# Layer A of a hybrid decoder step written out in TensorE's order

## The chip, the cores and the metric

The kernel runs as one program on one core of a Trainium2 chip. Its engines are TensorE (PE, with weight loads shown as PEld), VectorE (DVE), ScalarE (ACT), GpSimd (POOL) and SyncE (SP), which issues nearly all transfers between memory and the chip. The metric is the time of one execution on the device in microseconds (us), the median of the runs.

## The reference

One step of a two-layer decoder for a prompt of 272 positions (16 learned ones and 256 given) and 8 samples of one position. Layer A is RWKV-7 time mixing, layer B is sliding-window attention with a K/V shared from the stream after layer A. All is float32.

```python
prev = concat([shift_prev, xn[:, :-1]]); xx = prev - xn
xm = xn[:, :, None] + xx[:, :, None] * mu                       # six mixes of width 2048
r, k, v, z = einsum('btpd,pde->btpe', xm[:, :, :4], w_rkvz)      # 2048 x 4096 each
decay = exp(-exp(-softplus(-(w0 + tanh(xw @ w1) @ w2)) - 0.5)); a = sigmoid(a0 + (xa @ a1) @ a2)
kk = normalised(k * k_k); k = k * (1 + (a - 1) * k_a); b = kk * a
S = S * d - (S @ kk) b + v k; y = S @ r                          # scan over positions, 64 heads of 64
y = groupnorm(y) * gn_g + gn_b + sum(r * k * r_k) * v
h = x + (y * silu(z)) @ w_out                                    # 4096 x 2048
# layer B: shared K/V = rmsnorm(h) @ w_kv; q, z = rmsnorm(h) @ w_qz; attention with sinks;
# h = h + (att * silu(z)) @ w_o; out = rmsnorm(h)
```

## The kernel before, in words

A large product is computed as three products of rounded halves: weights and activations are split into a high part in TensorE's faster float32 form (fp32r) and the rest (`split`, L165: ACT makes the high part, DVE the rest), and `mm3` (L187) multiplies high by high, high by low and low by high. Weights come in pieces of 256 KB (`wunits`, L170: four raw buffers, five of each half); a piece serves 12 matmuls of 128 x 128 by 280 columns (272 prompt positions and 8 samples). A product here means one such sum for 256 output columns (`gemm`, L193): 8 pieces for 2048 inputs. Products go to one of three PSUM banks (`pm`).

The mixes for r, k, v and z are kept in memory (`md`), 8 tiles of 560 KB each, and loaded into a pool of 8 tiles (`load_mix`, L454). `proj` (L462) makes the products of one of r, k, v, z for some pairs of heads' blocks, evacuates them, and stores them to memory. k also gets the norms of its keys (`key_norms`), v is transposed.

Layer A has 64 heads, worked on in 16 units of four heads (u) and 8 double units (o). `prep` (L597) loads a unit's r, k, v, makes the decays and a (a small lora product each), and sends the samples' vectors to memory by a transpose (`ps_sm`, L664). `scores` (L707) makes the triangular products within chunks of 64 positions, `solve` (L769) inverts them in blocks (`ps_so`), `chain` (L838) passes the state through 5 chunks, each in three steps (ps_wu and ps_sy; the inverse, L888; the new state, L891 and L893), `group_norm` (L917) finishes y and stores it in `yd`. `decode` (L948) does the samples.

`phase_a` (L535) writes these in a loop over double units and puts the recurrence under `high_priority`; the products of the next group of heads (k, v and r, with three mix loads: nine in all, and one for z) stand between. Which instruction goes where on an engine is planned at build time by a scheduler that goes by simulated times and priorities, on TensorE too, so products and recurrence are interleaved by its plan. After the loop come the z products. For blocks below `GZ` = 14 pairs the z product is multiplied by y at once (L491 to L496); the last block is gated later (`gate_a`). `out_a1` (L1084) adds the first half of the output product (16 of 32 input tiles, blocks 0 to 3), with its gated y in mix tiles; `out_a` (L1107) loads and splits the late gates (`load_gated`, blocks 4 to 7) and does the second half. The scratch pool of the recurrence closes before `out_a` opens its own.

Of the kernel before, what the change touches and what calls it, by code (L numbers as in the profile page):

```python
# [8 lines left out]
F32 = mybir.dt.float32  # L9
# [20 lines left out]
LR = 96  # L30
HD = 64
NU = NP // 2
GZ = 14
# [65 lines left out]

class Kernel:  # L100
    def __init__(self, nc, tc, I, O):
        self.nc, self.tc, self.I, self.O = nc, tc, I, O

        self.raws, self.los = [], []

        self.wx = None
        self.plan = []

    def run(self):
        nc, tc = self.nc, self.tc  # L110
        import contextlib
        with contextlib.ExitStack() as st:
# [10 lines left out]
            with tc.tile_pool(name="stage", bufs=2) as self.sp:  # L123
                self.right = tc.tile_pool(name="mix", bufs=8, side="right")
                self.mp = self.right.__enter__()
                with tc.tile_pool(name="ph0", bufs=1) as self.ph:
                    self.phase0()
                with tc.tile_pool(name="rec", bufs=1, reuse_waits="tile") as self.rp:
                    self.phase_a()
            with tc.tile_pool(name="res", bufs=1, reuse_waits="tile") as self.op:  # L130
                self.right.__exit__(None, None, None)
                self.right = tc.tile_pool(name="kv", bufs=1, reuse_waits="tile", side="right")
                self.kvp = self.right.__enter__()
                self.right2 = tc.tile_pool(name="st0", bufs=1, reuse_waits="tile", side="right")
                self.st0 = self.right2.__enter__()
                self.right3 = self.tc.tile_pool(name="wx0", bufs=1, reuse_waits="tile", side="right")
                self.wx0 = self.right3.__enter__()
                with tc.tile_pool(name="gA", bufs=1, reuse_waits="tile") as self.gp:
                    self.out_a()
                with tc.tile_pool(name="B", bufs=1, reuse_waits="tile") as self.bp:  # L140
                    self.phase_b()
                with tc.tile_pool(name="gB", bufs=1, reuse_waits="tile") as self.gp:
                    self.out_b()
                self.wx = None
                self.right2.__exit__(None, None, None)
                self.right3.__exit__(None, None, None)
                self.g0.__exit__(None, None, None)
# [39 lines left out]
    def mm3(self, ps, wh, wl, xh, xl, start, stop):  # L187
# [3 lines left out]
        mm(ps, wl, xh, start=False, stop=stop)  # L191
# [95 lines left out]
    def phase0(self):  # L287
# [144 lines left out]
        self.xr0 = x(xr)  # L432
# [21 lines left out]
    def load_mix(self, m, nm):  # L454

        out = [self.mix_tile(f"{nm}_{g}") for g in range(8)]
        for t, d in zip(out, (self.md[m][g] for g in range(8))):
            self.nc.sync.dma_start(t.bitcast(F32), d)
        return lambda k: self.parts(out, k)


    def proj(self, m, x, pairs, dst, gemm=None):  # L462

        nc = self.nc
        for p0 in pairs:
# [5 lines left out]
            for j, ps in enumerate(pss):  # L471
                if m == 3:
                    th = self.sp.tile([128, N], F32, tag="sqp", bufs=1, name=f"th{p0}_{j}")
                    nc.scalar.activation(th, ps, AF.Tanh, scale=0.5)
                    nc.vector.scalar_tensor_tensor(t[:, j], th, 1.0, ps, op0=ALU.add, op1=ALU.mult)
                else:
                    nc.scalar.copy(t[:, j], ps)
                if m == 1:
                    sq = self.sp.tile([128, N], F32, tag="sqp", bufs=1, name=f"sqp{p0}_{j}")
                    nc.scalar.activation(sq, ps, AF.Square, scale=self.pcol(P_KK, p0 + j))  # L480
                    if j == 0:
                        pk = self.bank(self.py if p0 < 8 else self.pm, f"ps_kk{p0}")
                    nc.tensor.matmul(pk[:4, :N], self.sel[:, 4 * j:4 * j + 4], sq, start=j == 0, stop=j == 1)
                if m == 2:
                    pt = self.bank(self.pe if p0 < 8 else self.pm, name=f"ps_vt{p0}_{j}")
# [5 lines left out]
            if m == 3 and p0 < 2 * GZ:  # L491

# [345 lines left out]
    def chain(self, o):  # L838
# [17 lines left out]
        for q in range(2):  # L856
            G.memset(X[0][H(q), q], 0.0)
# [650 lines left out]
```

## Time and profile before

| | |
|---|---|
| median of 3 runs | 2351.3 us (2350.19 to 2351.96) |
| the profiled execution | 2355.23 us, of which the span from first to last instruction is 2352.6 us |
| busy share of the span | PE 96%, PEld 88%, DVE 73%, ACT 55%, POOL 3% |
| mean granted clock of TensorE | 0.981 |
| DMA | 464.71 MB, mean 198 GB/s |

Busy shares are means over stages. Layer A's products and recurrence lie between about 165 and 1410 us, the second output part and the shared K/V up to 1600, attention with the products of layer B from 1600 to 2100, the last product after that. Matmuls are pipelined: one of 280 columns is shown as about 0.29 us, and the next starts after less than half of that.

### The profile page before, as it was taken

How to read it: one execution, taken by the hardware profiler on the slowest of the kernel's cores; microseconds unless marked ns; L12 is line 12 of the kernel's file. 1: busy time of each engine (PE TensorE's matmuls, PEld its weight loads, DVE VectorE, ACT ScalarE, POOL GpSimd, SP SyncE). 2: the span in 40 equal slices, each digit the busy share in tenths (PEclk: the TensorE clock that was granted, in tenths of full speed). 3: DMA queues.
4: the chain of work that ended last, by engine and by line, in shares of the span. 5: the costliest groups of instructions: out<-in, count | busy, mean ns of one | idle time of the engine just before them, and what ended most of it. 6: DMA issues, size and time to landing. Idle time of an engine off the chain costs nothing.

```text
span 2352.6 us, 57011 instructions
## 1 busy us (share of the span) xinstructions
PE 2264.2 (96%) x21840; PEld 2069.3 (88%) x21840; DVE 1727.6 (73%) x4134; ACT 1299.4 (55%) x3042; POOL 63.5 (3%) x82
## 2 busy tenths in 40 slices
PE   7999999999999999999998999999999999999997
PEld 4898889888888888999898899999888899899997
DVE  5866768757785687876788567896777777688886
ACT  3556656665655766576554544564545445555443
POOL 0010000001000000000000000100000000000000
PEclk9999999999999999999999999999999999999999
DMA  7987667657586577855655568757343444356774
GB/s 251 327 262 255 208 211 250 214 184 248 150 244 213 167 230 226 258 172 155 196 168 163 168 193 263 242 185 224 108 129 117 144 131 137 110 170 219 233 226 148
DMA packets 425984, 464.71 MB, mean 198 GB/s; under 512 B 64472, under 2 KB 381336, under 8 KB 425320
## 3 DMA queue, kind: packets, MB, share of 16 engines
q1 hardware_dynamic: 424896, 458.79, 61.5%
q8 instruction: 171, 2.80, 0.5%
q10 hardware_dynamic: 816, 2.29, 0.3%
q14 instruction: 101, 0.83, 0.1%
HBM read 396.66 MB, written 68.44 MB: 198 GB/s over the span
## 4 chain that ended last, share of the span: by engine, by line
PE 83%; DMA 7%; DVE 5%; ACT 3%; issue 2%; SPq 0%; DVEq 0%; ACTq 0%
PE ps_z L189 6%; PE ps_z L190 6%; PE ps_z L191 6%; PE ps_q L191 3%; PE ps_q L189 3%; PE ps_q L190 3%; PE ps_ob L191 3%; PE ps_ob L190 3%; PE ps_ob L189 3%; PE ps_v L189 3%; PE ps_v L190 2%; PE ps_v L191 2%; PE ps_r L191 2%; PE ps_r L189 2%; PE ps_r L190 2%; PE ps_oa L191 2%
## 5 line engine op out<-in xcount | busy, mean ns | idle before, releaser
L167 ACT CAST whi_z<-raw_z 128x512 fp32r<-128x512 f32 x256 | 157.6, 619 | 151.0 <-PE ps_z L190 93.1
L168 DVE TENSOR_TENSOR wlo_z<-raw_z,whi_z 128x512 fp32r<-128x512 f32 x256 | 174.9, 691 | 72.3 <-ACT whi_z L167 64.0
L189 PE MATMUL ps_z<-mhlz,whi_z 128*128 128x280 f32 x512 | 153.5, 300 | 0.0
L190 PE MATMUL ps_z<-mhlz,whi_z 128*128 128x280 f32 x512 | 152.1, 298 | 0.0
L191 PE MATMUL ps_z<-mhlz,wlo_z 128*128 128x280 f32 x512 | 150.3, 297 | 0.0
L189 PE MATMUL ps_z<-bmh,whi_z 128*128 128x264 f32 x512 | 148.2, 291 | 0.0
L190 PE MATMUL ps_z<-bml,whi_z 128*128 128x264 f32 x512 | 148.0, 290 | 0.0
L191 PE MATMUL ps_z<-bmh,wlo_z 128*128 128x264 f32 x512 | 147.6, 292 | 0.0
L190 PE MATMUL ps_q<-bml,whi_q 128*128 128x264 f32 x512 | 147.4, 289 | 0.0
L189 PE MATMUL ps_q<-bmh,whi_q 128*128 128x264 f32 x512 | 147.3, 289 | 0.0
L191 PE MATMUL ps_q<-bmh,wlo_q 128*128 128x264 f32 x512 | 146.6, 289 | 0.0
L189 PE MATMUL ps_ob<-ghi,whi_ob 128*128 128x264 f32 x512 | 145.8, 286 | 0.3 <-ACT whi_ob L167 0.3
L191 PE MATMUL ps_ob<-ghi,wlo_ob 128*128 128x264 f32 x512 | 144.2, 285 | 1.7 <-DVE wlo_ob L168 1.7
L190 PE MATMUL ps_ob<-glo,whi_ob 128*128 128x264 f32 x512 | 145.6, 285 | 0.0
L167 ACT CAST whi_oa<-raw_oa 128x512 fp32r<-128x512 f32 x128 | 78.9, 621 | 91.1 <-PE ps_oa L190 57.0
L167 ACT CAST whi_q<-raw_q 128x512 fp32r<-128x512 f32 x128 | 78.6, 620 | 84.0 <-PE ps_q L190 57.2
L167 ACT CAST whi_ob<-raw_ob 128x512 fp32r<-128x512 f32 x128 | 79.0, 620 | 80.4 <-PE ps_ob L190 71.7
L168 DVE TENSOR_TENSOR wlo_oa<-raw_oa,whi_oa 128x512 fp32r<-128x512 f32 x128 | 86.6, 689 | 49.5 <-ACT whi_oa L167 46.9
L168 DVE TENSOR_TENSOR wlo_r<-raw_r,whi_r 128x512 fp32r<-128x512 f32 x128 | 87.2, 689 | 47.8 <-ACT whi_r L167 46.6
L189 PE MATMUL ps_k<-mhlk,whi_k 128*128 128x280 f32 x384 | 117.9, 308 | 3.1 <-issue 3.1
L167 ACT CAST whi_v<-raw_v 128x512 fp32r<-128x512 f32 x128 | 78.4, 619 | 71.8 <-PE ps_v L190 32.0
L189 PE MATMUL ps_r<-mhlr,whi_r 128*128 128x280 f32 x384 | 115.8, 303 | 1.9 <-ACT whi_r L167 1.7
(476 smaller groups left out, 7773.6 us busy)
## 6 DMA issues: line engine op xcount, KB each, us to landing
raw_k<-a_w_rkvz SPq DMA_DIRECT2D x128, 256.0 KB
raw_v<-a_w_rkvz SPq DMA_DIRECT2D x128, 256.0 KB
raw_r<-a_w_rkvz SPq DMA_DIRECT2D x128, 256.0 KB
raw_z<-a_w_rkvz SPq DMA_DIRECT2D x128, 256.0 KB
raw_oa<-a_w_out SPq DMA_DIRECT2D x128, 256.0 KB
raw_q<-b_w_qz SPq DMA_DIRECT2D x128, 256.0 KB
raw_z<-b_w_qz SPq DMA_DIRECT2D x128, 256.0 KB
raw_ob<-b_w_o SPq DMA_DIRECT2D x128, 256.0 KB
```

The costliest lines, as they stand in the source:

```text
L167: self.nc.scalar.copy(hi, src)
L168: return self.nc.vector.tensor_tensor(lo, src, hi.bitcast(F32), op=ALU.subtract)
L189: mm(ps, wh, xh, start=start, stop=False)
L190: mm(ps, wh, xl, start=False, stop=False)
L191: mm(ps, wl, xh, start=False, stop=stop)
```

## The change

The changed kernel writes layer A in the order that TensorE is to follow. `drive` holds TensorE's order by hand (`pe_order`) and counts half pieces: after each six product matmuls it looks at the streams `epilogues`, `main` (scores, solve and chain), `preps`, `decodes` and `late_gates`, plus group norms and even scores put aside. Each stream is a generator that gives the number of half pieces until its next visit, and a condition, and stands until both hold. The other engines are still planned by the scheduler; instructions of the side streams are queued on DVE behind the split of a recent weight piece.

- The products are a single stream: r for group 0, then r, k, v, then v, k, r, then r, k, v, then z, then the first output part. Neighbours with the same mix share it, so that mixes are loaded 7 times, not 10; tile h of the next mix is loaded after piece h of the last product that uses the old one.
- Weights are split three pieces ahead (`W`).
- In `prep` the lora products come ahead of the loads of r and k; v is loaded later; lora halves have two buffers.
- The mean and variance of the group norm are made in three parts within the chain (`variance`).
- `GZ` is 12, not 14: blocks 6 and 7 are gated late. The late gates are made in the stream `late_gates`, beside the first output part, in a pool that takes the place of the recurrence's early scratch.
- Pools are opened and closed by name; `res` lies on the right side, and `at` is made later.

```diff
-GZ = 14
+GZ = 12
-        for o in range(-1, NU // 2):
-            n = 2 * o + 2
-            if n < NU:
-                if n % 4 == 0 and n:
-                    self.proj_group(n // 4)
-                    self.decode(n // 4 - 1)
...
+        self.drive(self.products(), [self.epilogues(), self.main(), self.preps(), self.decodes(), self.late_gates()])
+    def drive(self, products, streams):
...
+        with self.pe_order():
+            while more or self.later or len(live) > 1:
+                for s in list(live):
+                    if s[1] <= self.pos and (s[2] is None or s[2]()):
+                        turn = self.tc.issue_after(self.los[-2].ins) if self.pos and s[0] not in now else \
+                            contextlib.nullcontext()
...
+                            with self.tc.high_priority(offset=2000 if s[0] is now[1] else 0), turn:
+                                w = next(s[0])
...
+                        s[1:] = [self.pos + w, need]
+                more = more and next(products, None) is not None
+                self.pos += 1
+    def main(self):
+        for o in range(-1, NU // 2):
+            n = 2 * o + 2
+            if o >= 0:
+                yield from self.chain(o)
+                self.mark('u', o)
+                self.side.append(self.group_norm(o))
+            if n < NU:
+                yield 0, self.after(0, ('p', n + 1), ('c', n))
+                self.load_x(o + 1)
+                self.prep_e(n + 1)
+                self.mark('e', n + 1)
+                yield from self.scores(n + 1)
+                yield from self.solve(o + 1)
+                self.mark('s', o + 1)
+    def products(self):
+        order = [(1, (0, 1, 2)), (2, (2, 1, 0)), (3, (0, 1, 2))]
...
+                while len(W) < 3:
+                    u = next(units, None)
...
+                for c in (0, 1):
+                    for k in (0, 1):
...
+                        self.last = self.mm3(ps[c][:, :N], wh[:, k, cs], wl[:, k, cs], xh, xl, k0 + k == 0,
+                                             k0 + k == KT - 1)
...
+                        if m < 4:
+                            mix[h] = self.mix_part(m, h, i)
+                        else:
+                            mix[h] = self.gated1(h, ys.pop(0))
...
+                    yield True
     prep:
+        for i, (hi, lo) in enumerate(ws):
+            for j in range(2):
+                yield 2 if i or j else 7, self.pp_free
...
+            yield 0, self.after(6, ('n', u // 4), *(('x', m, p0) for m in range(3)))
         kT = w("kT", 2)
         dma(kT, self.kd[b][:, sl])
...
+            yield 0, self.after(0, ('g', u // 2 - 2))
+        vT = w("vT", 4)
+        dma(vT, self.vd[b][:, sl])
...
+        yield 12, self.pp_free
+        ps = self.pp_bank(f"ps_sm{u}")
...
+            yield 3, self.pp_free
+            ps = self.pp_bank(f"ps_bo{j}_{u}")
     scores:
+            yield 4 if c0 else 8
...
+        yield 4
...
+            yield 3
     solve:
+        yield 24
...
+        yield 2
...
+        yield 5
...
+        yield 3
     chain:
+            yield (5 if c else 3), (None if c or not o else self.after(2, ('g', o - 1)))
...
+            yield 3
...
+            yield 3
...
+            if c % 2 or c == 4:
+                self.variance(o, c // 2)
+        yield 4
     group_norm:
+            yield 2 if j else 32
+    def late_gates(self):
+        yield 0, self.after(0, ('u', NU // 2 - 1), ('d', 3))
+        self.close("early")
+        self.gp = self.open("gA", reuse_waits="tile")
+        self.gates = []
+        for b in range(G1, 8):
+            yield (8 if b == G1 else 4), self.after(4, ('g', b))
+            self.gates.append(self.gate_tiles(self.gp, N, b, self.gate_a(b, self.gp)))
```

## Rows read from the trace of the kernel before

**Rows 1.** Clock by core: span in us and mean granted TensorE clock.
```profile
core 0: 2352.6 us, clock 0.981
```
**Rows 2.** Busy table of the page: us, share of span, instructions.
```profile
PE 2264.2 (96%) x21840; PEld 2069.3 (88%) x21840; DVE 1727.6 (73%) x4134; ACT 1299.4 (55%) x3042; POOL 63.5 (3%) x82
```
**Rows 3.** Table by stage: length, busy us by engine, clock, DMA share, GB/s.
```profile
core 0: us, PE busy (x) PEld busy (x) DVE busy (x) ACT busy (x) POOL busy (x), PEclk, DMA share, GB/s
165.00:1435.00 1270.00, 1220.78 (x13924) 1108.35 (x13924) 912.55 (x2000) 758.72 (x1780) 41.34 (x47) 0.97 0.65 206
182.00:1285.00 1103.00, 1070.11 (x12203) 965.44 (x12204) 820.31 (x1825) 681.58 (x1636) 41.34 (x47) 0.98 0.65 205
1285.00:1310.00 25.00, 15.99 (x415) 14.78 (x414) 14.52 (x36) 10.95 (x19) 0.00 (x0) 0.73 0.56 180
1310.00:1410.00 100.00, 97.76 (x1046) 92.59 (x1045) 56.53 (x102) 46.14 (x88) 0.00 (x0) 1.00 0.58 184
1410.00:1435.00 25.00, 20.69 (x144) 20.01 (x144) 14.84 (x27) 11.38 (x17) 0.00 (x0) 0.93 0.93 303
1600.00:2100.00 500.00, 498.31 (x3881) 444.55 (x3881) 360.43 (x1273) 252.01 (x664) 0.00 (x0) 0.99 0.44 136
```
**Rows 4.** PE's waits, 165 to 1435: releaser, us in total, times, longest.
```profile
PE ps_so L809 <- DVE TN L797: 6.6, 1, 6.6
...
PE ps_r L189 <- ACT whi_r L167: 3.9, 2, 2.2
PE ps_k L189 <- issue: 3.1, 1, 3.1
```
**Rows 5.** PE in order of time, 1280 to 1283: start, length, operation.
```profile
1280.08 0.29 PE L189 MATMUL ps_z<-mhlz,whi_z 128*128 128x280 f32 x1
...
1281.75 0.29 PE L190 MATMUL ps_z<-mhlz,whi_z 128*128 128x280 f32 x1
...
1282.35 0.40 PE L191 MATMUL ps_z<-mhlz,wlo_z 128*128 128x280 f32 x1
1282.59 0.29 PE L189 MATMUL ps_z<-mhlz,whi_z 128*128 128x280 f32 x1
```
**Rows 6.** Chain of waits, 1270 to 1310: start, us, what.
```profile
1285.78 3.64 DMA yd<-vT
1289.44 2.85 DMA yl<-yd
...
1298.97 2.62 DMA gy<-yd
...
1303.29 2.67 DMA gy<-yd
```
**Rows 7.** Chain of waits, 1395 to 1436.
```profile
1409.80 7.47 DMA raw_oa<-a_w_out
1417.34 7.92 DMA raw_oa<-a_w_out
```
**Rows 8.** Groups of DVE instructions by line: busy us, mean ns, idle before.
```profile
L168 DVE TENSOR_TENSOR wlo_oa<-raw_oa,whi_oa 128x512 fp32r<-128x512 f32 x68 | 46.2, 690 | 36.8 <-ACT whi_oa L167 35.0 <-PE ps_oa L191 1.2
L927 DVE SCALAR_TENSOR_TENSOR Y<-gmean,Y 128x1536 f32<-128x1536 f32 x8 | 14.0, 1744 | 0.0
L495 DVE SCALAR_TENSOR_TENSOR st<-st,yl 128x544 f32<-128x544 f32 x14 | 10.1, 722 | 2.8 <-DMA yl<-yd 2.6
L1068 DVE SCALAR_TENSOR_TENSOR gy<-gz,gy 128x280 f32<-128x280 f32 x4 | 1.6, 445 | 1.1 <-DMA gy<-yd 1.1
```
**Rows 9.** DMA issues by tile: count, KB each.
```profile
mhlk<-md SPq DMA_DIRECT2D x24, 560.0 KB
```
**Rows 10.** SP's queue: what it waited for, us, times, longest.
```profile
SPq L616 <- DVE llo L168: 17.6, 10, 5.5
```
**Rows 11.** One prep: a load's issue on SP, the transpose on PE.
```profile
1020.68 1.09 SPq L609 DMA_DIRECT2D rT<-rd  x1
...
1043.36 0.27 PE L664 MATMUL ps_sm<-consts,sm 128*96 128x128 f32 x1
```
**Rows 12.** One visit of scores on PE, and its last evacuation on DVE.
```profile
1107.62 1.16 PE L732 MATMUL ps_sc<-E,KB 64*128 64x128 f32 x14
...
1114.24 0.42 DVE L742 TENSOR_TENSOR RB<-ps_sc,consts 64x256 f32<-64x256 f32 x1
```

More of the change, by code (lines that the diff above doesn't have):

```diff
@@ L122, in run @@
             self.load_consts()
[L123 to L147, printed above, removed]
@@ new lines, in run @@
+            self.sp = self.open("stage", bufs=2)
+            self.mp = self.open("mix", bufs=8, side="right")
+            self.ph = self.open("ph0")
+            self.phase0()
+            self.close("ph0")
+            tile = dict(reuse_waits="tile")
+            pools = self.open("late", **tile), self.open("early", **tile)
+            self.rp = Pools(pools, "vT Y ev gmean gvar rsyy rsty")
+            self.phase_a()
+            self.close("mix")
+            right = dict(side="right", **tile)
@@ new lines, in mark, with after, pp_bank, pp_free @@
+    def mark(self, *k):
+        self.done[k] = self.pos
+    def after(self, n, *ks):
+        return lambda: all(k in self.done and self.pos >= self.done[k] + n for k in ks)
+    def pp_bank(self, name):
+        self.pp_pos = self.pos
+        return self.bank(self.pp, name)
+    def pp_free(self):
+        return self.pos >= self.pp_pos + 2
+    def epilogues(self):
+        while True:
+            while self.later:
+                yield from self.later[0]
+                self.later.pop(0)
+            yield 1
@@ new lines, in main, with preps @@
+                self.load_x(o + 1)
[4 more added lines that the diff above has]
+                self.mark('s', o + 1)
+    def preps(self):
+        for n in range(NU):
+            if n % 2 == 0 and n:
+                yield 0, self.after(0, ('e', n - 1))
+            yield from self.prep(n)
+            self.mark('p', n)
+            if n % 2 == 0:
+                self.prep_e(n)
+                self.side.append(self.even_scores(n))
@@ L857, in chain @@
             G.memset(X[0][H(q), q], 0.0)
+        self.X = X
+    def chain(self, o):
+        nc, rp = self.nc, self.rp
+        V, A, G = nc.vector, nc.scalar, nc.gpsimd
+        MU, AD = ALU.mult, ALU.add
+        dma = nc.sync.dma_start
+        us = [self.U[2 * o + i] for i in range(2)]
+        TT, PC = self.TT, us[0]['PC']
+        H = lambda q: slice(64 * q, 64 * q + 64)
+        X = self.X
         FS = rp.tile([128, 4, 64], F32, tag="FS", name=f"FS{o}")
@@ L1110, in out_a @@
         self.rb = op.tile([128, N], F32, name="rb")
[L1111 removed]
         pool = self.gp
[L1113 removed]
+        x = lambda k: (self.gates[k // 4][0][:, k % 4], self.gates[k // 4][1][:, k % 4])
         self.kvx = []
```

379 lines of the change are left out of this document (245 added, 134 removed).

## The prediction

> **What bounds the kernel now.** I read the whole-run views first and then narrowed. The clock by core says that one core runs 2352.6 us at a mean granted clock of 0.981 [rows 1]; the profiled execution took 2355.23 us, so 2.6 us lie around the span. The busy table gives PE 96% of the span [rows 2]: TensorE bounds the kernel, and the change removes none of its matmuls. It can therefore win only PE's idle time and the time in which PE runs at 1.2 GHz instead of 2.4.
>
> The table by stage shows where those are [rows 3]. The change touches 165 to 1435 us (the r products of layer A up to the first pieces of the second output part). PE is busy 1220.8 us of 1270 there: 49.2 us idle. The parts are 32.9 us in 182 to 1285, 9.0 in 1285 to 1310, 2.2 in 1310 to 1410, 4.3 in 1410 to 1435 and 0.8 before. The clock column gives the second loss; I count it only against busy time, so that nothing is counted twice: 2% of 1070.1 us is 21.4, 27% of 16.0 is 4.3, 7% of 20.7 is 1.4, together 27.1 us. At most 49.2 + 27.1 = 76.3 us can come back. DVE is busy 820.3 of 1103 us (74%) in the long stretch, so it is no bound of its own.
>
> The list of PE's waits says that this is many small stalls, not one [rows 4]: 6.6 us once for the triangular solve, then 2 to 3 us at a time for ScalarE's halves of the weights, or for nothing that the profile shows ("issue"). PE takes its matmuls in the order in which they were written, so a recurrence matmul that waits holds up products whose operands are ready: at 1287 PE stood 6.6 us for TN with products of the output part right behind.
>
> **The change part by part.**
>
> *Work of PE.* The order is new, the amount is not. Products of layer A from r on: 64 (4 + 36 + 16 + 8), each 8 pieces of two halves, 1024 half pieces of six matmuls. From 1280.08 to 1281.75 thirteen matmuls start, 0.128 us each [rows 5], so a half piece is 0.77 us and all are 789 us. They ran from 165 to 1410, 1245 us; what is over is recurrence and loss. The recurrence keeps its matmuls, in the same groups (one for each PSUM tile that it fills, 384 by the code), so the 0.11 us that the first product after a visit loses (0.24 us from 1282.35 to 1282.59, not 0.13 [rows 5]) is paid about as often: by my count of the distances in the diff, two visits fall on one half piece 37 times. A tenth more breaks or fewer is 4 us either way; I take none.
>
> *Does the recurrence end in time?* Counting the set distances: the first pair is ready at half piece 72, a solve with its scores takes 56 (22 + 34), a chain 57, eight pairs give 72 + 56 + 8 x 57 + 7 x 57 = 983 of 1024. The last group norm ends at 1022, the last late gate at 1026, two half pieces past the products. So the chain neither trails the products nor stretches them: PE's work sets the length, and what is late is what each visit finds unready.
>
> *The hole at 1285 to 1310* (9.0 + 4.3 = 13.3 us). Here the chain shows one store and three loads of gates in a row, 3.64, 2.85, 2.62 us and again 2.67, and the wait for TN [rows 6]. After the change the solve has 24 half pieces (24 x 0.77 = 18.5 us of products, more with other visits) and each gate of the first output part is prepared as its mix tile comes free in the last z product, 15 half pieces (11.6 us) before its use, from three staging buffers. I take 11 back, and bound it by 0 and 13.3.
>
> *The hole at 1410 to 1435* (4.3 + 1.4 = 5.7 us). Two weight loads landed after 7.47 and 7.92 us [rows 7] with DMA 93% busy at 303 GB/s [rows 3], because the gates' loads all start when the recurrence ends. Three of the four late gates now load earlier. The last one: its rows are stored after the visit at 1022 (3.64 us), loaded (2.62 [rows 6]), multiplied (4 x 0.445 [rows 8]) and split (two instructions, 3 us together, estimated from 0.690 us for 512 columns [rows 8] by the 1120 of a gate); that is 11.0 us, against two half pieces and 72 matmuls, 1.5 + 9.2 = 10.7 us, before PE wants it. I take 4 back, bounds -2 and 5.7.
>
> *GZ from 14 to 12.* One more block is gated late: 4 x 0.445 us of DVE and a 560 KB load more; two multiplications of 0.722 us [rows 8] and two loads fewer. It lies beside the first output part; without that cover it costs some 5 us at the end (1.8 + one load of 3).
>
> *Mix loads 10 to 7.* 24 loads of 560 KB go [rows 9], 13.8 MB or 67 us of DMA at the 205 GB/s of the long stretch [rows 3]. They are beside PE; on the path are only the waits after a mix change, the 3.1 us before ps_k and parts of ps_r's 3.9 [rows 4]. I count them in the next item.
>
> *The rest, 165 to 1285 and 1310 to 1410* (0.8 + 32.9 + 2.2 + 21.4 = 57.3 us). A second buffer for the lora halves takes 17.6 us of waiting from SP's queue [rows 10], behind which weight loads stand; splitting the group norm's 1.74 us vector operations in three [rows 8] lets an evacuation in earlier. What would be left? The nearest row is the attention stage, where attention's small matmuls break off the products all along and DVE is as busy (72%): 1.7 us idle and clock 0.99 in 500 us [rows 3], so 6.7 us lost in 500, 16 in these 1220. The other end is all 57 stay. I take 25 left, so 32 back, as the distances here are shorter than what the old order kept (below). New waits queue all products behind them on PE, then the weight buffers, then SP.
>
> *Sum.* 11 + 4 + 32 = 47 us: 2355.2 - 47 = 2308 in profiled terms. The median of the runs is 2351.3, 3.9 below the profiled one, so **2304 us**.
>
> **The rivals.**
>
> *A: visits come before their operands (slower).* Place: the transpose of a prep's sample columns (ps_sm). In the old order rT's load was issued at 1020.68 and ps_sm started at 1043.36, 22.7 us later [rows 11]. The diff leaves 12 half pieces between the loads and ps_sm in ten of the sixteen preps (the first four and the odd ones from the fifth on); at 1.17 us a half piece, visits included ((1245 - 47) / 1024), that is 14.0 us. If 22.7 are needed, PE stands 8.7 us ten times: 87 us, 2304 + 87 = **2391**. It decides from 4.7 us each (47 / 10). The scores point the same way: matmuls at 1107.62, their last evacuation ended at 1114.66 [rows 12], 7.0 us, where the new distance is 4 half pieces and the visit itself, 3.1 + 1.1 and about one other visit. Against it: the 22.7 us held the four lora products too, which the diff puts ahead of the loads, and DVE served a 1.74 us group norm before those evacuations.
>
> *B: the weights are late.* During a mix change eight tiles of 560 KB and eight weight pieces of 256 KB, 6.7 MB, go in 16 half pieces, 18.7 us: 357 GB/s, where the busiest stretch moved 303 [rows 3]. At 303 it takes 22 us, 3.3 us too long, seven times: 23 us, and 47 - 23 = 24 us come back, **2327**. For it: the 7.5 us landings at 303 GB/s [rows 7]. Against: seven such changes instead of ten, and the tiles have 15 half pieces.
>
> *C: the clock.* Every visit makes short gaps. If these, not the long waits, lower the clock, layer A runs at 0.93 as in 1410 to 1435 [rows 3]: 7% of 1200 us is 84 against 27 now, 57 lost and half of the idle, 25, won: 2351 - 25 + 57 = **2383**. The attention stage, broken off all along too, at 0.99 speaks against it [rows 3], and so does the hole of 1285 to 1310, where the low clock (0.73) stands beside one wait of 6.6 us. The Trainium skill has a rule for this case ("TensorE: Matmul & The Clock Gate", "A second HAM failure mode: psum-queue depth-cycling"): short idle times between groups of matmuls, as PE goes round the PSUM banks, are enough to make its clock swing between the two rates. By that rule the time would be this 2383; the attention rows disagree with it, and so C gets little.
>
> *D: the stalls only move*, and the sum is the old one: 2347 to 2356.
>
> **How the numbers follow.** Forecast 0.58 (2304, own range 2282 to 2320), A 0.18, B 0.17, C 0.03, D 0.04. 0.2% (4.7 us) is about what a measurement of this kernel tells from no change. Faster: forecast and B, 0.75; within: D, 0.04; slower: A and C, 0.21. Low end: all 76 us back, 2351 - 76 = 2275, and a us for the last gate. High end: part of A, waits of 6 us at ten visits (2304 + 60 = 2364). This leaves out the far half of A, and C, about 0.15 above, and little below.
>
> **What would show it.** Right: PE idle from r to the first output part under 20 us and clock 0.99, no hole before the first output part, 56 loads of mix tiles instead of 80, products in runs of six between visits. Wrong: ps_sm, ps_sc or ps_bk at the head of PE's waits with DVE or DMA as releaser (A); whi or wlo at each mix change (B); clock under 0.95 without waits over 1 us (C). A DVE busy over 85% there would mean that I picked the wrong bound.

## The result, and the profile after

The changed kernel takes 2329.9 us (median of 5 runs, 2326.8 to 2338.5), the kernel before in the same session 2350.3 (2347.0 to 2352.0): ratio 0.9922, 95% interval 0.9900 to 0.9945. It is faster, by 20 us where I had forecast 47. The profiled execution took 2326.8 us, the lowest of the five. Its clock by core and busy table, answering to [rows 1, 2]:

```profile
core 0: 2325.0 us, clock 0.984
```
```profile
PE 2214.2 (95%) x21840; PEld 2044.4 (88%) x21840; DVE 1733.9 (75%) x4168; ACT 1299.8 (56%) x3042; POOL 57.8 (2%) x82
```

The count of PE's instructions is the same, but PE is busy 50 us less. The table by stage says where; columns as in [rows 3], the stretches moved with the landmarks (first output part from 1263.6, was 1298.2; second from 1404.9, was 1430.9):

```profile
165.00:1405.00 1240.00, 1173.19 (x13919) 1084.99 (x13918) 916.47 (x2029) 759.37 (x1780) 35.73 (x47) 0.98 0.64 199
182.00:1250.00 1068.00, 1017.21 (x12173) 938.19 (x12172) 795.51 (x1767) 681.66 (x1631) 31.97 (x43) 0.98 0.64 199
1250.00:1275.00 25.00, 20.56 (x152) 19.11 (x151) 20.89 (x56) 12.60 (x25) 3.54 (x3) 0.93 0.64 196
1275.00:1375.00 100.00, 95.06 (x1314) 89.48 (x1313) 75.23 (x166) 45.77 (x88) 0.21 (x1) 0.95 0.57 184
1380.00:1405.00 25.00, 22.30 (x162) 20.62 (x161) 15.02 (x26) 9.79 (x16) 0.00 (x0) 1.00 0.84 258
1575.00:2075.00 500.00, 496.84 (x3903) 444.47 (x3902) 363.91 (x1278) 253.40 (x667) 0.00 (x0) 0.99 0.46 137
```

Idle time in layer A rose, from 49.2 us [rows 3] to 66.8. The gain is in the busy time: 1220.8 became 1173.2 for as many matmuls. So the forecast had its sign right and both of its halves wrong: it expected the idle time to shrink and the busy time to stay. That the sign came out right is luck. The list of PE's waits, which answers to [rows 4] (releaser, us in total, times, longest), has grown from 23 to 30 rows, and the longest single wait has come down from 6.6 to 3.9 us; these are the first five:

```profile
PE ps_so L1045 <- issue: 7.0, 5, 1.9
PE ps_bk L992 <- DVE RB L983: 6.2, 4, 3.3
PE ps_so L1039 <- DVE TN L1024: 5.7, 4, 2.4
PE ps_sc L974 <- DVE RB L967: 5.0, 6, 1.6
PE ps_so L1066 <- ACT ET L1061: 4.4, 4, 1.7
```

To see what made the busy time smaller I took every PE matmul from the first r product to the last of the first output part, and the time from its start to the next one's start. Up to 450 ns it counts under the kind of step, what is over 450 ns counts as a wait. (Each float32 matmul of the recurrence stands twice in the trace.)

| step | before: count, us | after: count, us |
|---|---|---|
| product to product | 5782, 800.9 | 5764, 804.5 |
| product to recurrence | 361, 76.6 | 380, 79.6 |
| recurrence to product | 361, 56.6 | 380, 50.2 |
| recurrence, on to another line | 436, 72.1 | 254, 36.7 |
| recurrence, same line | 6965, 219.2 | 7128, 212.2 |
| over 450 ns, the excess | 41, 40.9 | 63, 55.7 |
| sum | 1266.4 | 1238.8 |

Half of the time in the row "another line" is gone: 182 such steps fewer, 35.4 us. Of the old 436 steps 263 also changed the shape of the matmul (rows x columns of its weights), 50.9 us, of the new 254 only 93, 16.2 us: 170 of the 182 steps that went, and 34.7 of the 35.4 us, are changes of shape. All steps up to 450 ns give 42.4 us, the waits take 14.8 back, and 27.6 are left. What lies outside this stretch takes as long as before (1086.2 and 1086.1 us). The median gives 20 instead of 28, since this profiled run lies 3 us below its median and the one of before 5 above.

The granted clock of the whole run goes against the change. It was 0.977 to 0.984 (median 0.980) in the five runs of the changed kernel, and 0.980 to 0.987 (median 0.984) in the 70 runs of the kernel before that stand beside the experiments (two more, at 0.91 and 0.71, left out). Among the runs of either kernel 0.001 less goes with some 1.7 us more, so an estimated 7 us of the gain are lost there. The profiled pair (0.984 and 0.981) does not show it.

What such a step is, PE's timeline of the kernel before shows (start, length, operation, count): a visit of the scores (ps_sc) is cut into three by the third step of a chain (ps_sy), and the chain's step into two.

```profile
1097.77 0.94 PE L732 MATMUL ps_sc<-E,KB 64*128 64x128 f32 x12
1098.64 0.28 PE L893 MATMUL ps_sy<-X,RB 16*16 16x64 f32 x2
1098.85 0.48 PE L732 MATMUL ps_sc<-E,KB 64*128 64x128 f32 x2
1099.27 0.62 PE L893 MATMUL ps_sy<-X,RB 16*16 16x64 f32 x14
1099.81 0.69 PE L891 MATMUL ps_sy<-X,BK 128*64 128x64 f32 x16
1100.43 0.48 PE L732 MATMUL ps_sc<-E,KB 64*128 64x128 f32 x2
1100.84 0.40 PE L190 MATMUL ps_z<-mhlz,whi_z 128*128 128x280 f32 x1
```

Two pieces of ps_sc that were cut off (two rows of the trace each) take 0.42 and 0.41 us up to the next start, twelve in a row 0.87, together 1.70. In the changed kernel, in whose order a visit can't be cut, all 16 take 1.09 us up to the next start:

```profile
1102.08 1.16 PE L957 MATMUL ps_sc<-E,KB 64*128 64x128 f32 x16
1103.17 0.40 PE L208 MATMUL ps_z<-mhlm,whi_z 128*128 128x280 f32 x1
```

### The profile page after: what moved, and what is told of

It is laid out like the page before. It is cut to its first block, busy times and chain, and to the rows that moved or that the text cites. A ratio compares the mean times of both kernels' runs of the same rounds, so it can differ in the third digit from the quotient of the medians.

```text
span 2325.0 us, 56966 instructions
## 1 busy us (share of the span) xinstructions
PE 2214.2 (95%) x21840; PEld 2044.4 (88%) x21840; DVE 1733.9 (75%) x4168; ACT 1299.8 (56%) x3042; POOL 57.8 (2%) x82
## 4 chain that ended last, share of the span: by engine, by line
PE 80%; DMA 7%; DVE 6%; ACT 4%; issue 2%; SPq 1%; DVEq 0%; ACTq 0%
PE ps_z L208 5%; PE ps_z L209 5%; PE ps_z L210 5%; PE ps_q L208 3%; PE ps_q L210 3%; PE ps_q L209 3%; PE ps_ob L210 3%; PE ps_ob L209 3%; PE ps_ob L208 3%; PE ps_k L208 3%; PE ps_v L208 3%; PE ps_r L208 2%; PE ps_v L209 2%; PE ps_v L210 2%; PE ps_k L210 2%
## 5 line engine op out<-in xcount | busy, mean ns | idle before, releaser
L208 PE MATMUL ps_z<-mhlm,whi_z 128*128 128x280 f32 x512 | 162.5, 317 | 2.6 <-DVE st L757 2.6
L209 PE MATMUL ps_z<-mhlm,whi_z 128*128 128x280 f32 x512 | 152.8, 298 | 0.0
L210 PE MATMUL ps_z<-mhlm,wlo_z 128*128 128x280 f32 x512 | 152.7, 298 | 0.0
L186 ACT CAST whi_ob<-raw_ob 128x512 fp32r<-128x512 f32 x128 | 79.0, 620 | 81.0 <-PE ps_ob L209 66.8
L187 DVE TENSOR_TENSOR wlo_v<-raw_v,whi_v 128x512 fp32r<-128x512 f32 x128 | 87.3, 686 | 47.7 <-ACT whi_v L186 42.7
L208 PE MATMUL ps_v<-mhlm,whi_v 128*128 128x280 f32 x384 | 121.8, 317 | 0.0
L208 PE MATMUL ps_k<-mhlm,whi_k 128*128 128x280 f32 x384 | 119.0, 310 | 0.0
L187 DVE TENSOR_TENSOR wlo_k<-raw_k,whi_k 128x512 fp32r<-128x512 f32 x112 | 77.3, 693 | 55.2 <-ACT whi_k L186 54.7
```

Of the source, the lines that this page charges most:

```text
L186: self.nc.scalar.copy(hi, src)
L187: return self.nc.vector.tensor_tensor(lo, src, hi.bitcast(F32), op=ALU.subtract)
L208: mm(ps, wh, xh, start=start, stop=False)
L209: mm(ps, wh, xl, start=False, stop=False)
L210: return mm(ps, wl, xh, start=False, stop=stop)
```

## The experiments

All times are medians of 4 to 12 runs; the ratio is to the kernel before, run beside them. The changed kernel itself stands at 0.9922 (0.9900 to 0.9945).

| run | us | ratio, 95% interval |
|---|---|---|
| e13_alternate_shapes | 2363.9 | 1.0040 (1.0025 to 1.0055) |
| e1_split | 2356.5 | 1.0019 (1.0006 to 1.0033) |
| e6_no_decode | 2348.9 | 0.9981 (0.9968 to 0.9994) |
| e14_alternate_same | 2337.6 | 0.9922 (0.9902 to 0.9942) |
| e7_solve_parts | 2332.1 | 0.9911 (0.9893 to 0.9928) |
| e3_mix10 | 2330.9 | 0.9908 (0.9893 to 0.9923) |
| e4_gates_after | 2331.4 | 0.9906 (0.9886 to 0.9926) |
| e8_variance_whole | 2330.8 | 0.9901 (0.9885 to 0.9918) |
| e5_hold2 | 2329.8 | 0.9900 (0.9883 to 0.9917) |
| e11_small_reader | 2325.7 | 0.9888 (0.9868 to 0.9907) |
| e9_tuned | 2319.8 | 0.9870 (0.9853 to 0.9887) |
| e12_spread | 2318.6 | 0.9853 (0.9811 to 0.9896) |
| e2_distances | 2316.1 | 0.9852 (0.9836 to 0.9868) |
| e10_tuned_hold1 | 2309.7 | 0.9822 (0.9802 to 0.9843) |

**What does a break cost?** First, visits cut in two with products between the parts:

```diff
                     mm(wu[R(q), 0, j], E(j, q)[:, 128 * c:128 * c + n], x[:, q, j], start=True, stop=True)
-
-                for j, q in heads:
...
-            yield 3
+            yield 1
+            with self.pe_order():
+                for j, q in heads:
...
+            yield 2
```

> The changed kernel with 112 of its recurrence visits cut in two, one half piece of products between the parts, the sum of the distances kept: per chunk of the chain ps_wu apart from ps_sy (40 times) and the new state's two halves apart (40), each set of ten transposes ps_bk apart (32). Theory 1, a break of TensorE's stream has a price of its own: in the changed kernel's trace a step from product to recurrence takes 207 ns from start to start, back 131, two products 136, and the steps replaced 52 (ps_wu to ps_sy), 152 (BK to RB) and about 30 ns (ps_bk). That is 0.15, 0.05 and 0.17 us a cut, 6 + 2 + 5.5 = 13.5 us: 2330 + 13.5 = 2343, ratio to the kernel before 0.997, with PE's idle over 450 ns as it was (55.7 us). Theory 2, breaks are free and the time follows the waits alone: 2330, ratio 0.992 within 0.002. If single parts come before their operands, the waits over 450 ns grow and say so.

It is 23 us slower than the changed kernel by the two ratios, 26 by the medians; I had worked out 13.5. PE went from products to recurrence 468 times instead of 380, so one more such break costs 23 / 88 = 0.26 us or 26 / 88 = 0.30; by the steps of the trace (both crossings 161.8 us, was 129.8) it is 0.36. The clock hides part of it: e1's runs had a median of 0.983 against 0.980, an estimated 5 us. The waits did not grow (53.2 us). Cutting visits is enough to lose the whole gain.

But breaks from products are not what the change saved; there are 19 more of them than before. So the next two kernels add steps between recurrence lines alone, 240 each, at the same places among the products. The first alternates matmuls of 128 and of 64 rows:

```diff
-                for i, f in enumerate((grow, of_u) if c < 4 else (of_u, grow)):
-                    for j, q in heads:
-                        f(j, q, i == 1 and j == 3)
+                for j in range(4):
+                    for i, f in enumerate((grow, of_u) if c < 4 else (of_u, grow)):
+                        for q in range(2):
+                            f(j, q, i == 1 and j == 3)
```

> The changed kernel with the two halves of the chain's third step written out alternately, two matmuls of 128 rows (BK), two of 64 rows (RB), and so on, instead of eight and eight: 7 changes of line instead of 1 in each of 40 visits, 240 more, at the same places among the products. Theory 1, going from one group of short matmuls to another costs PE time of its own: in the changed kernel's trace the step from BK to RB is 152 ns from start to start, within a group 30 on average, so 240 x 0.12 = 29 us, 2359, ratio to the kernel before 1.004; 2345 if only one direction of the change pays. Theory 2, what was won lies elsewhere, a change of line is free: 2327 to 2334, ratio 0.991.

The second does the same to the chain's first step, where both lines have 128 rows and 64 columns in four of the five chunks:

```diff
-                for j, q in heads:
-                    mm(wu[R(q), 0, j], E(j, q)[:, 128 * c:128 * c + n], x[:, q, j], start=True, stop=True)
+                for j in range(4):
+                    for q in range(2):
+                        mm(wu[R(q), 0, j], E(j, q)[:, 128 * c:128 * c + n], x[:, q, j], start=True, stop=True)
+                    for q in range(2):
...
```

> The changed kernel with the chain's first step written out alternately in the same way, two matmuls into ps_wu, two into ps_sy, both of 128 rows and 64 columns: also 240 more changes of line, without a change of shape. Theory 1a, the price is that of a change of shape (the step from ps_wu to ps_sy is 52 ns in the trace, as between pairs within a group): 2327 to 2334, ratio 0.991. Theory 1b, the price is that of a change of PSUM tile: as e13_alternate_shapes, 2345 to 2359.

The ratios are 1.0040 and 0.9922: the first loses 28 us against the second (1.18% of 2350), the second nothing by the ratio, whose interval is 5 us either way; its median, 2337.6, lies above the expected 2327 to 2334. PE's timeline of one visit in each, e13 first: with a change of shape a group of four takes 0.26 to 0.27 us, without one 0.11 (0.17 right behind a product).

```profile
329.53 0.34 PE L1135 MATMUL ps_sy<-X,BK 128*64 128x64 f32 x4
329.80 0.33 PE L1137 MATMUL ps_sy<-X,RB 64*64 64x64 f32 x4
330.06 0.34 PE L1135 MATMUL ps_sy<-X,BK 128*64 128x64 f32 x4
```
```profile
335.42 0.34 PE L1118 MATMUL ps_wu<-X,E 128*64 128x64 f32 x4
335.59 0.29 PE L1121 MATMUL ps_sy<-X,E 128*64 128x64 f32 x4
335.70 0.29 PE L1118 MATMUL ps_wu<-X,E 128*64 128x64 f32 x4
```

Over all visits the median step is 152 ns from BK to RB and 148 back, but 52 ns between ps_wu and ps_sy in either direction, which is also the step between pairs within a group. The last chunk, of 16 positions, is an exception that I had overlooked in e14: its weights have 16 columns for ps_wu and 48 for ps_sy, and there the same two lines take 149 ns in either direction. So 48 of e14's 240 added steps do change the shape, and 192 do not. Neither the change of line nor that of the PSUM tile costs, the change of the matmul's shape does: 0.12 us by e13 and the changed kernel (28 / 240), 0.15 by e13 and e14 (28 / 192). The Trainium skill has this rule ("TensorEngine Tiling (Array Packing)", "Key Properties"): changing the tiling mode, as opposed to the tile, drains the engine. It gives no price; these two runs agree with it. In the kernel before, visits of different shape cut into each other; the 170 changes of shape that went are 20 to 25 us at this price, of the 42, and the rest is spread over the other rows of the table. That the old order's cuts cost what e13's do I did not try in the old kernel itself.

**Do the waits come from short distances?** Distances moved from the chain (its first two steps) to the solve (groups 1, 2 and 4) and to the scores (the last group and the first ps_bk), in this order:

```diff
-            yield (5 if c else 3), (None if c or not o else self.after(2, ('g', o - 1)))
+            yield (4 if c else 3), (None if c or not o else self.after(2, ('g', o - 1)))
...
-            yield 3
+            yield 2
...
-        yield 24
+        yield 28
...
-        yield 2
+        yield 4
...
-        yield 3
+        yield 4
...
-        yield 4
+        yield 5
...
-            yield 3
+            yield 3 if j else 4
```

> The changed kernel with distances moved from the chain, whose steps were found ready 1.7 to 3 us early (5 to 4 and 3 to 2 half pieces), to the solve (24 to 28, 2 to 4, the last 3 to 4) and the scores (last 4 to 5, first ps_bk 3 to 4); a double unit is as long as before. Theory 1, the waits at ps_so (18.8 us), ps_bk (6.7) and ps_sc (5.3) come from distances that are short by 1 to 3 us and cost their full length: at least 20 of these 31 us go, 2310, ratio 0.983. Theory 2, the waits only move, to the shortened chain (ps_wu, ps_sy) or to weights behind them: 2325 to 2335, ratio 0.989 to 0.994. If the chain's steps then wait in most of their 40 visits, slower than 2335.

2316.1 us, 14 less (16 by the ratios), between the two theories. The waits aimed at went (ps_sc 5.0 to 1.7 us, ps_bk 6.2 to 1.1; the solve's first and fourth groups are no longer in the list), but the sum over 450 ns stayed (56.6 us), and others came up. Its first two waits:

```profile
PE ps_so L1057 <- DVE TN L1052: 8.2, 4, 3.3
PE ps_z L208 <- DVE st L757: 7.6, 6, 3.1
```

The third group of the solve had not waited before. Where the 14 us lie is open: the waits are as long as before, and the profiled run, the slowest of the four (2322.2), shows only 5.3 us less in the steps up to 450 ns (1177.8, with 14 breaks fewer). The clock of e2's runs was 0.983 to 0.985, that of the changed kernel's 0.977 to 0.984, which by the estimate above is some 7 us; whether the distances raised it is not shown.

e9 takes these on as well (the first line is the solve's third group, a line like the second stands for v's transposes, and the chain's first step goes from 3 to 1):

```diff
-        yield 5
+        yield 7
...
-                yield 2 if i or j else 7, self.pp_free
+                yield (3 if u > 1 else 2) if i or j else 7 if u else 12, self.pp_free
...
-                        self.evacuate(P, c, ps[c][:, :N])
+                        with self.tc.high_priority(offset=2000):
+                            self.evacuate(P, c, ps[c][:, :N])
```

> e2_distances (2316) with the waits of its own trace taken on in turn: the solve's third group at 7 half pieces instead of 5 (TN2, 8.2 us), paid for by the chain's first step (3 to 1); the first lora product at 12 instead of 7 (lhi, 3.9 us) and later ones 3 apart (cl and ta, 7.2 us); v's transposes 3 apart (vk, 4.9 us); evacuations of products ahead on VectorE and ScalarE (ps_z for st, 7.6 us). Theory 1, each wait costs its length and longer distances remove it: 20 of these 32 us go, 2296, ratio to the kernel before 0.977. Theory 2, with a wait gone the next link of the same chain of operands is late, as TN2 was when the stalls of the second group went: 2310 to 2316, ratio 0.983 to 0.985, and the waits over 450 ns stay above 45 us. Rival: evacuations ahead of the weight halves make whi and wlo late: slower than e2_distances.

2319.8, no better than e2. The waits at TN2 and lhi went, that at vk fell from 4.9 to 1.1 us, but the one at ps_z for st, for which the evacuations were put ahead, rose from 7.6 to 12.7 us, and others came up (52.9 us in all).

**Can visits share breaks?** Side streams are held back until the main stream has a visit too, by up to two half pieces on the changed kernel (e5), by up to one on e9 (e10):

```diff
-                for s in list(live):
+                held = ('e', 1) in self.done and any(s[0] is now[1] for s in live)
+                met = False
+                for s in sorted(live, key=lambda s: s[0] is not now[1]):
+                    if held and s[0] is not now[1] and not met and s[1] + 2 > self.pos:
+                        continue
                     if s[1] <= self.pos and (s[2] is None or s[2]()):
+                        met = True
```

> The changed kernel with the side streams held back by up to two half pieces until the scores, solve or chain visit too, so that more visits share one break; by counting the distances 72 of 347 breaks go. Theory 1, the price is that of leaving and re-entering the products, as the cuts of e1_split cost it (26 us for 112, 0.23 us each): 72 x 0.23 = 17 us less, 2314, ratio to the kernel before 0.984. Theory 2, a visit that follows another costs nearly as much as a break of its own (in the trace 143 ns from one recurrence line to another, against 207 + 131 - 136 = 202 for a break): 72 x 0.06 = 4 us less, 2326, ratio 0.989. Rival: two visits in a row crowd ScalarE and VectorE and the waits eat it: 2330 or slower.

> e9_tuned with the side streams held for up to one half piece to share a break with the main stream; by counting 349 places with visits become 307. Theory 1, a shared break saves what the trace says (about 60 ns): 2.5 us less than e9_tuned. Theory 2, 0.23 us each as a cut cost in e1_split: 10 us less. Theory 3, as in e5_hold2: nothing, since crowded visits give it back in waits.

e5 made no difference (2329.8): 57 breaks from products fewer (323), but 59 more steps between recurrence lines, so that the steps up to 450 ns gave little (1181.7 us, was 1183.1). Its stalls without a releaser, of which more below, took 16.0 us instead of 7.0:

```profile
PE ps_so L1050 <- issue: 16.0, 7, 4.4
```

e10 is 10 us faster than e9 for 36 breaks fewer (338, was 374), nearer to 0.23 us each than to 60 ns, though it too has 38 more steps between recurrence lines (300). At 2309.7 it is the fastest kernel here, 20 us below the changed one (24 by the ratios). In the trace the steps give only 4.3 of these 10 us (1175.1 to 1170.8), the waits 2.3, and 2.5 lie outside layer A, so that the price of a break is not shown by e10. Its clock, a median of 0.984, is also higher than e9's (0.982) and the changed kernel's (0.980).

**Is VectorE too busy?** e6 takes the samples' sums over the state away from it; e11 does the same and has the added line, one small reader of each piece:

```diff
-            for w, o in ((kk, sa), (dr, y)):
-                tt(T, S, rowb(w), op=MU)
-                V.reduce_sum(o[:, iq], T, axis=AX.X)
+            V.tensor_copy(sa[:, iq], S[:, :, 0])
```

> The changed kernel without the samples' sums over the state (128 VectorE operations of 0.684 us, 87.5 us of the 916 in layer A, are left out). Theory 1, the waits of over 450 ns (55.7 us in layer A) come from VectorE's queue: evacuations stand behind such work, so the waits for its results (RB, TN, st, ET: about 20 us) lose at least half, 2318 to 2320, ratio 0.987. Theory 2, the operands' own chain is longer than the distance, whoever else uses VectorE: no change, 2327 to 2333, ratio 0.991.

> e6_no_decode again, with one small VectorE operation left on each piece of state, so that its 256 KB loads stay as far apart as in the changed kernel (in e6_no_decode all 32 of a group went at once between 220 and 330 us, and products stood for weights). What is left out: the samples' sums over the state, about 85 us of VectorE's 916 in layer A. Theory 1, the waits come from VectorE's queue: they fall by 10 us or more of 55.7, 2320 or less, ratio 0.986. Theory 2, they come from the operands' own chain: 2327 to 2333, ratio 0.990 to 0.992, as the part of e6_no_decode after 340 us already says (its stretch up to the second output part took as long as the changed kernel's).

e6 was slower than the changed kernel, by 19 us (14 by the ratios), which neither theory held. Without a reader nothing spaced the loads of the state: 32 instead of 2 went between 200 and 340 us, and SP's queue, in which the weights stand too, waited for them:

```profile
SPq L1234 <- DMA dS<-state_wkv: 37.6, 22, 4.7
```

e11 is the clean form: 4 us less (8 by the ratios, whose intervals still touch) for 70 us less of VectorE's busy time (1664.0, was 1733.9), the waits 51.3 instead of 55.7 us. So VectorE's load makes a small part of the waits. For one kind e10's VectorE timeline shows what does, from 714 to 719 us: eight instructions in a row for a later visit (the four long ones here), one of the samples' sums, the split of two lora halves, and only then the copy ET, for which PE stood 3.7 us from 715.1 on.

```profile
714.28 0.68 DVE L922 TENSOR_TENSOR KB<-kT,cl 128x512 f32<-128x512 f32 x1
714.99 0.68 DVE L924 TENSOR_TENSOR KB<-ta,cl 128x512 f32<-128x512 f32 x1
715.69 0.68 DVE L930 TENSOR_TENSOR E<-kk,Pp 128x512 f32<-128x512 f32 x1
716.29 0.68 DVE L931 TENSOR_TENSOR E<-rT,Pp 128x512 f32<-128x512 f32 x1
717.70 0.75 DVE L187 TENSOR_TENSOR llo<-lraw,lhi 96x256 fp32r<-96x256 f32 x2
718.37 0.41 DVE L1047 COPY ET<-ps_so 128x256 f32<-128x256 f32 x1
```

So in e12 this burst is written out in four parts, one half piece apart:

```diff
-                self.prep_e(n)
+                yield from self.prep_e(n)
...
+        yield 1
         tt(KB[:, :, 0:4, 0:64], ch(a), ch(cl), op=MU)
```

> e10_tuned_hold1 (2310) with the even units' decayed keys and receptances (KB and E, ten VectorE instructions, 3.5 us in a row) written out in four parts, one half piece apart, instead of at once. In e10's trace each of these bursts but one stands ahead of the copy of the solve's first group (ET), which was ready 1 to 3 us before: PE waited there 5 times, 12.3 us. Theory 1, what a visit waits for is the order of VectorE's queue, not its load (e11_small_reader took 85 us of load away for 4 us of time): the ET waits fall to under 5 us and the time by 5 to 8 us, 2303, ratio to the kernel before 0.979. Theory 2, another piece of side work takes the place ahead of ET, or the next link is late: 2308 to 2312, ratio 0.982, waits over 450 ns in all as in e10 (50.6 us).

The ET waits went, 12.3 us to none among the first twenty rows, as theory 1 said. The time did not fall with them (2318.6, and 1222.5 us for layer A against 1221.4): the next link of the same solve was late. PE's waits, e10 and then e12:

```profile
PE ps_so L1051 <- DVE ET L1047: 12.3, 5, 4.3
```
```profile
PE ps_so L1066 <- DVE TN L1061: 9.8, 3, 4.5
```

Beyond layer A e12 was 7.6 us longer than e10 (1094.0 and 1086.4); that part is not explained.

**Stalls without a releaser.** The first wait of the changed kernel, "issue", lies inside a group:

```profile
299.05 1.26 PE L1039 MATMUL ps_so<-TN,Noff 32*32 32x16 f32 x128 [0.93 <-DVE TN L1024]
301.98 1.03 PE L1045 MATMUL ps_so<-TR,ET 32*16 32x16 f32 x102
304.91 0.39 PE L1045 MATMUL ps_so<-TR,ET 32*16 32x16 f32 x26 [1.90 <-issue]
```

```diff
         for i in range(16):
+            if i == 8:
+                yield 2
             for q in Q:
```

The second group has the same.

> The changed kernel with the first two groups of the solve (128 short matmuls each, 12 product matmuls between them) cut in two each, two half pieces of products between the parts; paid for by the chain's first step (5 to 4). Theory 1, the stalls inside the second group for which the profile shows no reason (4 to 5 times, 0.7 to 3.8 us, 8 to 13 us in all in the four runs with these distances, always near the same matmul) come from so many short instructions in a row: they go, at a price of 16 cuts of 0.23 us: 2330 - 8 + 4 = 2326, ratio 0.990, no such stall over 400 ns left. Theory 2, they wait for something else: they stay, and the cuts make it 2334, ratio 0.993.

As theory 1 said, the stalls are gone: one of 0.96 us is left. The time is not lower (2332.1). The steps up to 450 ns took 5.2 us more (1188.3), about the price set for the cuts, and the sum of the waits stayed (55.2 us): the third group's TN2, which had not waited before, now heads the list.

```profile
PE ps_so L1061 <- DVE TN L1056: 8.1, 4, 2.7
```

The other runs fit: with two half pieces between the solve's first two groups the stalls in the second took 7.0 to 16.0 us (the changed kernel and the nine runs that keep its distance there), with four 0.2 to 3.8 (e2, e9, e10, e12).

**The parts that I had costed at nothing or at a few us.** Mixes loaded more often in the same order, late gates written behind the first output part, mean and variance in one go over all 1536 columns (e3, e4, e8):

```diff
-            if nxt != P['m']:
+            if nxt != P['m'] or i in (3, 19, 31):
...
-        yield 0, self.after(0, ('u', NU // 2 - 1), ('d', 3))
+        yield 0, lambda: self.pos >= 1024 and self.after(0, ('u', NU // 2 - 1), ('d', 3))()
...
-            if c % 2 or c == 4:
-                self.variance(o, c // 2)
+            if c == 4:
+                self.variance(o, 0)
```

> The changed kernel with its products in the same order, but with the mix loaded anew where two neighbouring groups share it (after the first r, v and r groups): 10 loads of eight tiles instead of 7. Theory 1, the loads lie beside TensorE: no change, 2328 to 2333, ratio 0.991 to 0.993. Theory 2, part of the gain came from fewer loads: each extra change costs what ps_r and ps_k waited before (7 us for two kinds), so 3 x 3 = 9 us, up to the 67 us of traffic if nothing hides it: 2339 or more, ratio 0.995 or more, with ps_r or ps_v at the head of the waits.

> The changed kernel with its four late gates started only when the first output part has ended, instead of beside it. Theory 1, the gates were hidden there: PE now stands for the first gate's loads, multiplications and splits (about 3 + 2 + 3 us) and then for part of the next three, 10 to 20 us: 2340 to 2350, ratio 0.996 to 1.000, in a hole before ps_oa. Theory 2, the gates are quick enough from a free DMA queue, so that only the first is seen: 2335 to 2338. No change at all would say that the place of the gates is worth nothing.

> The changed kernel with mean and variance of the group norm made in one go after the chain, as before the change, instead of in three parts within it. Theory 1, the long VectorE operations (1.7 us each) hold up evacuations: 8 times 2 to 4 us at the scores or the next chain, 2346 or more, ratio 0.997. Theory 2, the distances there have the room (the next scores come at 8 half pieces): no change, 2327 to 2334.

None moved the time, but two of the edits do less than their texts say. e3 loads the mix anew at one place, not at three: behind products 19 and 31 the mix changes anyway (v to k, r to k), and the trace has 64 tiles, not 80 (the changed kernel's line first, then e3's):

```profile
mhlm<-md SPq DMA_DIRECT2D x56, 560.0 KB
```
```profile
mhlm<-md SPq DMA_DIRECT2D x64, 560.0 KB
```

One load of eight tiles more costs nothing that shows; the 3 us that theory 2 set for one are within the noise, and three more were not tried. In e4 the splits of the gates came later (the first at 1403.5 us, was 1371.6), but still before the first output part ended at 1408.0, and the loads of the first two gates stayed where they were (1371, was 1366). So e4 shows that splits some 30 us later (5 for the last gate) cost nothing, and does not decide between its theories. In e8 the long vector operations have the room that theory 2 gave them.

## Why the prediction was wrong

- **Work of PE: wrong, and the largest error.** I took the breaks "paid about as often" and their change as 0, with 4 us for a tenth more or fewer. I had counted groups by the code, 384 in both kernels, as if they ran whole in the old one. They did not: 436 steps from one recurrence line to another became 254, 170 of those that went were changes of shape, and the steps up to 450 ns fell by 42.4 us. e13 and e14 show that a change of shape between groups has a price, e1 that a break from products has. The rows at 1097.77 stood in the trace of before.
- **The rest of the stage: wrong, with the opposite sign.** I expected 32 of 57.3 us back, going by the attention stage [rows 3]. The idle time of the long stretch rose from 32.9 us in 1103 to 50.8 in 1068; the clock column, 0.98 in both, gave 1 us. Attention was the wrong neighbour: the solve is a chain of copies and small matmuls with fixed distances, and what is not ready holds up all products. This is rival A's mechanism, but not at its place: ps_sm did not wait, the solve, the scores and ps_bk did for VectorE and ScalarE, 21 times, at most 3.3 us at a time, 23.0 us in all (11.7 before the change), not 87.
- **Why the waits stayed.** e2, e7, e9 and e12 each removed most of the waits that they aimed at, and the sum over 450 ns stayed between 49 and 57 us. In e2, e7 and e12 the next link of the solve was late. So the 14 us of e2 are not waits that went. VectorE's load is at most a small part of the cause (e11); in e10 its order was the cause, for ET, but putting that right gained nothing either.
- **The hole before the first output part: moved.** Of 13.3 us, 5.9 are left in 1250 to 1275 (4.4 idle, 7% of 20.6 by the clock), but the next 100 us lose 9.7 where they lost 2.2 [rows 3]. I expected 11 back; the two together give none.
- **The hole before the second part: less than I took.** 2.7 us are left of 5.7 in 1380 to 1405, but the next 25 us lose 1.8 where they lost none, nearly all of it at 1416 for the last gate's halves (ghi, glo), which I had put at 11.0 us against 10.7. I had taken 4 back; about 1.2 came.
- **The end of the recurrence, GZ, the mix loads: right as far as tried.** The first output part began 35 us earlier, the chain's last step came at 1361 us, 44 before the first output part's end, the stretch after it is as long as before, 56 loads stand in the trace as expected, and one load of eight tiles more cost nothing that shows (e3).
- **Rivals B, C, D.** PE waits 4.0 us for whi in the very first r products (191 to 215 us) and 2.3 near the end of the first output part, at no change of mix: B fell. The clock is 0.98 with more breaks from products than before, and the runs with 338 and 468 breaks (e10, e1) have 0.984 and 0.983: C fell, and with it, for this kernel, the clock rule that I cited; the 0.004 that the changed kernel's runs lie below the old one's are an estimated 7 us, not 57. D, that stalls only move, fell too: they grew by 15 us, and the time fell all the same.

## What to carry to other kernels

When an order written by hand replaces a planner's, count in the old trace how often short groups cut into each other, and price a change of matmul shape (0.12 to 0.15 us here) and a break of a product stream (0.26 to 0.36 us) before looking at idle time; PE's busy share hides both. A longer distance to one visit did not lower the sum of the waits here; lengthening one link showed the next. Fewer, shared breaks on top of the longer distances gave the best version, 2309.7 us.

## What the runs showed of the hardware

- Among short matmuls of 64 columns a step is 7 ns within a pair and 52 between pairs (medians), whichever PSUM tile they write; where their shape changes between 128 and 64 rows it is 148 to 152 ns, and where it changes between 16 and 48 columns 149 (e13, e14).
- PE may run out of instructions. Ahead of each of the changed kernel's five stalls inside the solve's second group a packet of the queue that the profile calls "instruction" starts, 0.4 to 1.9 us before, and takes 1.0 to 1.2 us. The DMA of that kernel from 302.3 to 304.9 us, the stall shown above (queue, packets, MB, share):

```profile
q1 hardware_dynamic: 433, 0.92, 96.2%
q8 instruction: 1, 0.02, 2.9%
```

  The whole run has 171 such packets, 2.80 MB, 64 bytes for each of PE's 43680 matmuls and weight loads, so that a packet would be 256 instructions if this queue serves PE alone; the solve's first two groups hold 512, with 12 products between. Four of the stalls lay at the same matmul, within two, in e3, and spreading the groups ended them (e7). That the packets are the reason was not tried by itself. The Trainium skill ("Runtime: NRT & Kernel Launch", "Instruction fetch mechanics") has it that such loads are hidden, because instructions are dispatched more slowly than they arrive. If the packets are the reason, it does not hold here, with a short matmul every 10 ns (102 in 1.03 us) and the DMA engines 96% busy with other packets.
- Taking work away made a kernel 14 to 19 us slower (e6): the reader of a buffer was what spaced its loads in SP's queue.
